# A hybrid retention, DeltaNet and MoE block on one core: where the first expert's conversions and the shared expert's chunks stand in the order of issue

## The chip, the cores and the metric

The kernel runs on one core of a Trainium2 chip, as one launch. The metric is the device time of that core in microseconds; lower is better. The engines are TensorE (PE; weight loads are shown as PEld), VectorE (DVE), ScalarE (ACT), GpSimd (POOL) and SyncE (SP), each with an in-order queue of its own.

## The reference

One layer over 512 latent tokens of width 1024, with 256 context tokens. A token mixer (retention and gated DeltaNet) comes first and ends in a projection by `w_o`. Then follows a mixture of experts, the part that the change touches:

```python
scores = jax.nn.sigmoid((xt @ w_router_l).astype(jnp.float32))
...                                   # 4 of 8 groups kept, then the 8 best of 64 experts per token
slot_tok = jnp.full((n_slots,), t, jnp.int32).at[slot].set((order // TOP_K).astype(jnp.int32))
...
def expert_block(args):
    xe, e = args
    return (jax.nn.silu(xe @ w_gate_l[e]) * (xe @ w_up_l[e])) @ w_down_l[e]
...
shared = (jax.nn.silu(xt @ w_sh_gate_l) * (xt @ w_sh_up_l)) @ w_sh_down_l
return (routed + shared).reshape(b, l, d)
```

So each token goes to 8 of 64 experts (width 256) and to one shared expert (width 256); the two results are added, normed and added to the stream.

## The kernel before

Everything up to about 600 us is the token mixer. `phaseO` then does the last projection and the routing, in four tiles of 128 tokens. `proj(us, t, c)` (L1081) multiplies with `w_o`; `post(t)` (L1094) norms the tile on DVE, POOL and ACT into `h2`; `turn(t)` (L1112) transposes `h2` on TensorE (L1117), copies it to `h2T` on ACT (L1118) and calls `router(t)` (L1006): 8 matmuls (L1010), a sigmoid on ACT (L1012), then some 30 short DVE steps that end in the 0/1 selection `sel` (L1034) and the weights `wt`, which SP writes to DRAM. After every second tile `router` also transposes two selections into `selT` on TensorE (L1043).

The shared expert is done in four chunks of 128 tokens. `shared_up(t)` (L1051) is 32 matmuls on TensorE (64 records, L1056), a Silu on ACT (L1059) and a product on DVE (L1060); `shared_down(t)` (L1062) is 4 matmuls (8 records, L1067), two copies on ACT (L1068) and a DMA on the ACT queue. Chunk 0 runs in `phaseO`, chunks 1 to 3 in `phaseM`.

`phaseM` first places the lists: from `selT` and a table `left`, eight rounds of max and replace on DVE (L1193, L1195) give the first slots of every expert for two halves of the tokens; two copies put the halves into `both` (L1197 on ACT, L1198 on DVE), one small matmul brings them together (L1200) and DVE writes the token indices `slots` (L1202). With them `prepare(e)` gathers the tokens of an expert with an indirect DMA on POOL (L1214).

The weights of an expert come as three loads of 1 MB on the SP queue (L1178). Gate and up lie in a ring of six buffers (three experts); two of the six are the memory of `h2T`, and the third `w_down` buffer is that of the shared expert's `w_sh_down`, so that these come free only when the shared expert is done. A gate or up matrix is converted: `conv` (L1153) casts it on ACT into a high part `wh` (L1156) and subtracts on DVE into a low part `wl` (L1158); seven such buffers exist. `convert(e, n)` (L1263) does this for matrix n of expert e and then issues the load of expert e + 3 into the buffer that has come free. `make(e, part)` transposes the gathered tokens (L1222, with L1224 on ACT and L1225 on DVE). The loop over 64 experts (L1402) then does for each: the gate projection (L111 to L113), a conversion for the next expert, the transposes of the activations of the one before (L1242), the up projection, another conversion, the next `make`, `down` (L1253) with a scatter on POOL (L1258), and the next gather.

The order on each engine is not quite the order of the program text: a planner goes through the program with times of its own and may issue an instruction earlier than an earlier one in the text, if its inputs and buffers are free by its reckoning. So the three conversions that stand ahead of the loop in the text (experts 0, 0 and 1) and one from inside the loop run, in part, among the steps of `phaseO`. `tc.issue_after(ins)` is an order to that planner: every instruction made inside the block that runs on the engine of `ins` is queued behind `ins`; it puts no wait on the chip, and other engines are not bound by it.

Of the kernel before, what the change touches and what calls it, by code (L numbers as in the profile page):

```python
# [9 lines left out]
F32 = mybir.dt.float32  # L10
# [3 lines left out]
AF = mybir.ActivationFunctionType  # L14
OP = mybir.AluOpType
# [56 lines left out]
class K:  # L72
# [903 lines left out]
    def phaseO(self):  # L976
        nc, tc, a = self.nc, self.tc, self.a
        tt = nc.vector.tensor_tensor
        ts = nc.vector.tensor_scalar
# [7 lines left out]
        p = rt = self.pool("op", side="right", es=es, reuse=True)  # L987
# [10 lines left out]
        sc, cand, sel, wt, posm, rep, selb = G("scr"), G("cand"), G("sel"), G("wt"), G("posm"), G("rep"), G("selb", BF)  # L998
# [7 lines left out]
        def router(t):  # L1006

            ps = self.pi()
            for k in range(8):
                nc.tensor.matmul(ps[:, 0:64], self.h2T[:, k, t * 128:t * 128 + 128], wr[:, k], start=k == 0, stop=k == 7)  # L1010
            s, c = sc[:, t], cand[:, t]
            nc.scalar.activation(s, ps[:, 0:64], AF.Sigmoid)  # L1012
            tt(c, s, bias, op=OP.add)
            for g in range(8):
                nc.vector.max(t8[:, g], c[:, g * 8:g * 8 + 8])
            gs, kp, kb, m8, sm = [sm8[:, t, i * 8:i * 8 + 8] for i in range(5)]
            tt(gs, t8[:, :, 0], t8[:, :, 1], op=OP.add)
            i0 = gs[:, None, :].to_broadcast([128, 8, 8])
            i1 = gs[:, :, None].to_broadcast([128, 8, 8])
            tt(A, i0, i1, op=OP.is_gt)  # L1020
            tt(B, i0, i1, op=OP.is_equal)
            f = lambda x: x.rearrange("p g h -> p (g h)")
            tt(f(B), f(B), cons["glt"], op=OP.mult)
            tt(A, A, B, op=OP.add)
            nc.vector.tensor_reduce(kp, A, axis=AX.X, op=OP.add)
            ts(kp, kp, 3.5, None, op0=OP.is_lt)
            ts(kb, kp, -1.0, 1e30, op0=OP.add, op1=OP.mult)
            c3 = c.rearrange("p (g e) -> p g e", g=8)
            b8 = lambda x: x[:, :, None].to_broadcast([128, 8, 8])
            tt(c3, c3, b8(kp), op=OP.mult)  # L1030
            tt(c3, c3, b8(kb), op=OP.add)
            nc.vector.max(m8, c)
            nc.vector.match_replace(rep[:, t], m8, c, -3e30)
            tt(sel[:, t], rep[:, t], c, op=OP.not_equal)  # L1034
            tt(wt[:, t], s, sel[:, t], op=OP.mult)
            nc.vector.tensor_reduce(sm[:, 0:1], wt[:, t], axis=AX.X, op=OP.add)
            nc.vector.reciprocal(sm[:, 0:1], sm[:, 0:1])
            ts(wt[:, t], wt[:, t], sm[:, 0:1], 2.5, op0=OP.mult, op1=OP.mult)
            nc.vector.tensor_copy(selb[:, t], sel[:, t])
            nc.sync.dma_start(self.h2d[t * 128:t * 128 + 128, 1024:1088], wt[:, t])  # L1040

            if t % 2:
                nc.tensor.transpose(self.selT[:, t // 2 * 128:t // 2 * 128 + 128], sel[:, t - 1:t + 1].rearrange("p c e -> p (c e)"), self.ident)  # L1043


        b1, k0_ = self.hxpool.tile([128, 2, 8, 256], F32, name="wsh", tag="b1"), self.keep.tile([128, 2, 1024], F32, name="wshd", tag="k0")
        wsh = [b1[:, 0], b1[:, 1], k0_]
# [3 lines left out]
        def shared_up(t):  # L1051
            ts_ = slice(t * 128, t * 128 + 128)
            ps = self.pi()
            for j in range(4):
                for k in range(8):
                    nc.tensor.matmul(ps[:, j * 128:j * 128 + 128], wsh[j // 2][:, k, j % 2 * 128:j % 2 * 128 + 128], self.h2T[:, k, ts_],  # L1056
                                     start=k == 0, stop=k == 7)
            sg = sgs[t] = mp.tile([128, 256], F32, name="shg", bufs=2)
            nc.scalar.activation(sg, ps[:, 0:256], AF.Silu)  # L1059
            tt(sg, sg, ps[:, 256:512], op=OP.mult)  # L1060

        def shared_down(t):  # L1062
            y = self.rawp.tile([128, 1024], F32, name="y", tag="raw")
            for c in range(2):
                ps = self.pa()
                for k in range(2):
                    nc.tensor.matmul(ps, sgs[t][:, k * 128:k * 128 + 128], wsh[2][:, k, c * 512:c * 512 + 512], start=k == 0, stop=k == 1)  # L1067
                nc.scalar.copy(y[:, c * 512:c * 512 + 512], ps)  # L1068
            nc.scalar.dma_start(self.accd[0][t * 128:t * 128 + 128], y)

        self.shared = lambda t: (shared_up(t), shared_down(t))

        wo = a["w_o"][0].rearrange("(k p) n -> p k n", p=128)
# [38 lines left out]
        def turn(t):  # L1112
            for cc in range(2):
                ps = self.pi()
                for k in range(4):
                    kk = cc * 4 + k
                    nc.tensor.transpose(ps[:, k * 128:k * 128 + 128], h2s[t][:, kk * 128:kk * 128 + 128], self.ident)  # L1117
                nc.scalar.copy(self.h2T[:, cc * 4:cc * 4 + 4, t * 128:t * 128 + 128], ps.rearrange("p (k n) -> p k n", k=4))  # L1118
            router(t)
# [7 lines left out]
        for t in range(4):  # L1127
            proj(us, t, 1)
            post(t)
            if 0 < t < 3:  # L1130
                turn(t - 1)
        shared_up(0)
        turn(2)
        turn(3)
        shared_down(0)
        z = self.rawp.tile([128, 1024], F32, name="zero", tag="raw")
        nc.gpsimd.memset(z, 0.0)
        for t in range(4):
# [4 lines left out]
    def phaseM(self):  # L1143
        nc, tc, a = self.nc, self.tc, self.a
        tt = nc.vector.tensor_tensor
        ts = nc.vector.tensor_scalar
        p, cons, sel, selb, wt, posm = self.mp, self.cons, self.sel, self.selb, self.wt, self.posm
# [5 lines left out]
        def conv(w, eng, n):  # L1153
            h, l = T8("wh"), T8("wl")
            for i in range(0, 2048, max(n, 1024)):
                nc.scalar.copy(h[:, i:i + max(n, 1024)], w[:, i:i + max(n, 1024)])  # L1156
            for i in range(0, 2048, n):
                eng(l[:, i:i + n], w[:, i:i + n], h[:, i:i + n].bitcast(F32), op=OP.subtract)  # L1158
            return h, l
# [8 lines left out]
        raw = lambda e, n: DW[e % 3] if n == 2 else GU[(2 * e + n) % 6]  # L1168

        def load(e, n, wix=None):  # L1170
            if e > NE:
                return
            t = raw(e, n)
            if e == NE:
                wix = self.xtra[0] if wix is None else wix
                nc.gpsimd.indirect_dma_start(t[:, :], None, wf[NAMES3[n]], bass.IndirectOffsetOnAxis(ap=wix[:, :1], axis=0))
            else:
                nc.sync.dma_start(t, a[NAMES3[n]][0, e].rearrange("(p k) f -> p (k f)", p=128))  # L1178
# [2 lines left out]
            load(e, n)  # L1181


        lf = self.rawp.tile([128, 448], F32, name="left", tag="raw")
        left, first, both = lf[:, 0:256], lf[:, 256:320], lf[:, 320:448]
        o = self.coff["left"][0]
        nc.scalar.dma_start(left, a["cst"][:, o:o + 256])
# [2 lines left out]
        slots = p.tile([128, 64], I32, name="slots")  # L1190
        for r in range(8):
            e8 = first[:, r * 8:r * 8 + 8]
            nc.vector.max(e8, left)  # L1193
            if r < 7:
                nc.vector.match_replace(left, e8, left, 0.0)  # L1195

        nc.scalar.copy(both[0:64, 0:64], first[0:64])  # L1197
        nc.vector.tensor_copy(both[64:128, 64:128], first[64:128])  # L1198
        ps = self.pi()
        nc.tensor.matmul(ps[:, 0:64], both, cst("i2"), start=True, stop=True)  # L1200

        ts(slots, ps[:, 0:64], -1.0, 512.0, op0=OP.mult, op1=OP.add)  # L1202
        for t in range(1, 4):
            self.shared(t)
        xg6, xg3 = q.tile([128, 3, 1088], F32, name="xg", bufs=1), self.hxpool.tile([128, 3, 1088], F32, name="xg", tag="b1")
        xgs = [x[:, i] for x in (xg6, xg3) for i in range(3)]
        for x in xgs:
# [55 lines left out]
        def convert(e, n):  # L1263
            if e <= NE:
                cv[e, n] = conv(raw(e, n), tt, 2048)
                load(e + 3, n)
# [3 lines left out]
        def prepare(e):  # L1270

            if e > NE:
                return
            if e < NE:
                SL[e] = slots[:, e:e + 1]
            else:
                SL[e], W[e] = self.xtra[1:]
            XG[e] = gather(SL[e])
            if e < NE:
                W[e] = XG[e][:, 1024 + e:1025 + e]  # L1280
# [7 lines left out]

        for e in range(3):
            prepare(e)  # L1290
        convert(0, 0)
        convert(0, 1)
        convert(1, 0)
        for e in range(2):
            make(e, 0)
            make(e, 1)
# [8 lines left out]
        ps = self.pi()  # L1305
# [10 lines left out]
        for t in range(4):  # L1316
            s = slice(t * 64, t * 64 + 64)
# [166 lines left out]
```

## Time and profile before

| what | us |
|---|---|
| median of 3 runs | 1450.79 (1450.4 to 1452.89) |
| the profiled execution | 1450.15 |
| its span, first to last instruction | 1448.4 |
| TensorE busy | 1338.8 (92% of the span) |
| DVE busy | 901.3 (62%) |
| ACT busy | 655.7 (45%) |
| POOL busy | 404.1 (28%) |

The busy shares are means over stages that differ: the mixer to about 600 us, the routing from there to about 736 us, the expert loop to about 1413 us, and the last sums. The rows below come from the routing and from the loop. A timeline row gives the start, the duration of the merged instructions, engine, line, operation, the tile written and those read, and the count; in brackets stands how long the engine was idle before it, and which instruction ended that. A granted clock of 1.00 is 2.4 GHz and 0.50 is 1.2 GHz.

### The profile page before, as it was taken

What the parts mean: (1) busy time and instruction counts of PE and PEld (TensorE: products, weight loads), DVE (VectorE), ACT (ScalarE), POOL (GpSimd) and SP (SyncE); (2) the same over time, 40 slices, a digit from 0 to 9 for tenths busy, and PEclk for the clock granted to TensorE, in tenths of its full rate; (3) what the DMA queues carried; (4) which work ended last, traced back from release to release, by engine and by line L of the source; (5) the groups of instructions that cost most, each with busy time, mean ns of one, the idle gap of its engine ahead of it and who ended that gap; (6) DMA issues with size and microseconds to landing.
All of it is one profiled execution on the core that took longest, in us unless ns stands there. A gap on an engine that the chain in (4) does not pass through costs nothing.

```text
span 1448.4 us, 20720 instructions
## 1 busy us (share of the span) xinstructions
PE 1338.8 (92%) x7848; PEld 1085.2 (75%) x7848; DVE 901.3 (62%) x1268; ACT 655.7 (45%) x927; POOL 404.1 (28%) x330
## 2 busy tenths in 40 slices
PE   6989888899999999997799999999999999999991
PEld 2668776898887767776678787878787878888770
DVE  5635695566777556557366666666666666666543
ACT  5534442543323223244145655555555555555531
POOL 0414644855330000012022222222222222223312
PEclk9899999999999999999899999999999999999995
DMA  8643421102226578566388999999999999999954
GB/s 283 191 106 107 125 58 41 44 16 84 78 69 203 177 212 232 167 248 245 136 282 295 351 364 347 367 354 347 364 357 361 362 362 357 368 353 353 327 184 124
DMA packets 138841, 340.51 MB, mean 235 GB/s; under 512 B 28218, under 2 KB 84574, under 8 KB 113780
## 3 DMA queue, kind: packets, MB, share of 16 engines
q1 hardware_dynamic: 110952, 289.46, 56.5%
q0 software_dynamic: 19584, 38.99, 10.7%
q10 hardware_dynamic: 8204, 10.72, 2.4%
q8 instruction: 63, 1.03, 0.3%
q14 instruction: 38, 0.31, 0.1%
HBM read 326.59 MB, written 48.31 MB: 259 GB/s over the span
## 4 chain that ended last, share of the span: by engine, by line
PE 66%; DVE 8%; DMA 8%; POOL 2%; issue 2%; ACT 1%; SPq 0%; ACTq 0%; DVEq 0%; POOLq 0%
PE cs L1253 15%; PE acc L113 12%; PE acc L112 12%; PE acc L111 12%; PE ci L1222 4%; DMA raw<-in_w_in_dram 2%; PE ci L1056 2%; DMA wd<-in_w_down_dram 2%; DVE wu L107 1%; PE acc L1242 1%; PE acc L1067 1%; DMA mraw<-in_w_mod_dram 1%; ACT wu L100 1%; PE ci L596 1%; PE cs L655 1%
## 5 line engine op out<-in xcount | busy, mean ns | idle before, releaser
L111 PE MATMUL acc<-wh,xT 128*128 128x256 f32 x1040 | 304.9, 293 | 0.0
L113 PE MATMUL acc<-wh,xT 128*128 128x256 f32 x1040 | 294.4, 283 | 0.0
L112 PE MATMUL acc<-wl,xT 128*128 128x256 f32 x1040 | 294.1, 283 | 0.0
L1158 DVE TENSOR_TENSOR wl<-w,wh 128x2048 fp32r<-128x2048 f32 x88 | 201.6, 2291 | 87.4 <-PE acc L112 86.0
L1253 PE MATMUL cs<-wd,aT 128*128 128x512 f32 x520 | 235.8, 596 | 2.9 <-DMA wd<-in_w_down_dram 2.1
L1258 POOL DMA_INDIRECT acc<-y,slots x64 | 101.9, 1592 | 474.7 <-ACT y L1255 427.4
L1156 ACT CAST wh<-w 128x2048 fp32r<-128x2048 f32 x88 | 167.3, 1901 | 100.7 <-PE acc L113 85.6
L111 PEld LDWEIGHTS acc<-wh,xT 128*128 128x128 f32 x1040 | 199.6, 192 | 0.2 <-issue 0.2
L112 PEld LDWEIGHTS acc<-wl,xT 128*128 128x128 f32 x1040 | 199.4, 192 | 0.2 <-issue 0.2
L113 PEld LDWEIGHTS acc<-wh,xT 128*128 128x128 f32 x1040 | 198.8, 191 | 0.0
L1253 PEld LDWEIGHTS cs<-wd,aT 128*128 128x128 f32 x520 | 94.5, 192 | 97.6 <-issue 96.6
L1225 DVE TENSOR_TENSOR xT<-ci,xT 128x512 fp32r<-128x512 f32 x130 | 89.1, 686 | 89.7 <-ACT xT L1224 89.6
L100 ACT CAST wu<-raw 128x1024 fp32r<-128x1024 f32 (+1 forms) x73 | 74.9, 1036 | 113.4 <-DMA raw<-in_w_in_dram 74.1
L1158 DVE TENSOR_TENSOR wl<-wgu,wh 128x2048 fp32r<-128x2048 f32 x42 | 96.3, 2292 | 41.5 <-PE acc L112 41.4
L111 PE MATMUL acc<-hTx,wu 128*128 128x512 f32 (+1 forms) x296 | 119.2, 403 | 1.9 <-ACT wu L100 1.9
L113 PE MATMUL acc<-hTx,wu 128*128 128x512 f32 (+1 forms) x296 | 118.4, 400 | 1.5 <-DVE wu L107 1.5
L112 PE MATMUL acc<-hLx,wu 128*128 128x512 f32 (+1 forms) x296 | 117.9, 398 | 0.0
L107 DVE TENSOR_TENSOR wu<-raw,wu 128x1024 fp32r<-128x1024 f32 (+1 forms) x61 | 77.1, 1270 | 64.6 <-ACT wu L100 63.5
L1156 ACT CAST wh<-wgu 128x2048 fp32r<-128x2048 f32 x42 | 79.7, 1898 | 50.0 <-PE acc L113 42.1
L1222 PEld LDWEIGHTS ci<-ident,xg 128*128 128x128 f32 x520 | 73.4, 192 | 29.8 <-issue 29.5
L1214 POOL DMA_INDIRECT xg<-h2d,slots x64 | 71.3, 1113 | 31.6 <-issue 18.0
L1222 PE MATMUL ci<-ident,xg 128*128 128x128 f32 x520 | 80.0, 278 | 0.0
(492 smaller groups left out, 2371.6 us busy)
## 6 DMA issues: line engine op xcount, KB each, us to landing
wd<-in_w_down_dram SPq DMA_DIRECT2D x64, 1024.0 KB
w<-in_w_gate_dram SPq DMA_DIRECT2D x43, 1024.0 KB
w<-in_w_up_dram SPq DMA_DIRECT2D x43, 1024.0 KB
raw<-in_w_in_dram SPq DMA_DIRECT2D x56, 512.0 KB
wgu<-in_w_gate_dram SPq DMA_DIRECT2D x21, 1024.0 KB
wgu<-in_w_up_dram SPq DMA_DIRECT2D x21, 1024.0 KB
mraw<-in_w_mod_dram SPq DMA_DIRECT2D x32, 512.0 KB
wm<-in_w_mod_dram SPq DMA_DIRECT2D x16, 512.0 KB
```

The source lines that it names most:

```text
L100: nc.scalar.copy(dst, src)
L107: (self.nc.gpsimd if eng == "pool" else self.nc.vector).tensor_tensor(dst, src, hi.bitcast(F32), op=OP.subtract)
L111: mm(out, ah, bh, start=start, stop=False)
L112: mm(out, ah, bl, start=False, stop=False)
L113: mm(out, al, bh, start=False, stop=stop)
L1156: nc.scalar.copy(h[:, i:i + max(n, 1024)], w[:, i:i + max(n, 1024)])
L1158: eng(l[:, i:i + n], w[:, i:i + n], h[:, i:i + n].bitcast(F32), op=OP.subtract)
L1214: nc.gpsimd.indirect_dma_start(xg[:, :], None, self.h2d[:, :], bass.IndirectOffsetOnAxis(ap=ix, axis=0), bounds_check=511, oob_is_err=False)
L1222: nc.tensor.transpose(ps[:, k * 128:k * 128 + 128], xv[:, :, c * 4 + k], self.ident)
L1225: tt(l, ps, h.bitcast(F32), op=OP.subtract)
L1253: nc.tensor.matmul(ps, aT[:, m], wd[:, s], start=k == 0, stop=k == 1)
L1258: nc.gpsimd.indirect_dma_start(self.accd[acc][:, :], bass.IndirectOffsetOnAxis(ap=sx, axis=0), y[:, :], None, bounds_check=511, oob_is_err ...
```

## The change

In `phaseO` the transposes of the selections are taken out of `router` into `turn_sel`. `shared_up(1)` now follows `shared_down(0)`; the two `turn_sel` are queued on TensorE behind its last matmul, and `shared_down(1)` follows. In `phaseM` `shared(2)` stands between the eight rounds and the copies into `both`; the first of these copies moves from ACT to DVE. The table `left` moves from the ring `raw`, which the shared expert's results use too, to a buffer `k1`. `shared(3)` and the three conversions ahead of the loop stand in a block whose ACT instructions are queued behind the last router's sigmoid and whose DVE instructions are queued behind the writing of `slots`; `shared(3)` stands behind the first of the conversions.

```diff
@@ -1009,7 +1009,7 @@
             for k in range(8):
                 nc.tensor.matmul(ps[:, 0:64], self.h2T[:, k, t * 128:t * 128 + 128], wr[:, k], start=k == 0, stop=k == 7)
             s, c = sc[:, t], cand[:, t]
-            nc.scalar.activation(s, ps[:, 0:64], AF.Sigmoid)
+            self.scored = nc.scalar.activation(s, ps[:, 0:64], AF.Sigmoid)
             tt(c, s, bias, op=OP.add)
             for g in range(8):
                 nc.vector.max(t8[:, g], c[:, g * 8:g * 8 + 8])
@@ -1039,8 +1039,9 @@
             nc.vector.tensor_copy(selb[:, t], sel[:, t])
             nc.sync.dma_start(self.h2d[t * 128:t * 128 + 128, 1024:1088], wt[:, t])
 
-            if t % 2:
-                nc.tensor.transpose(self.selT[:, t // 2 * 128:t // 2 * 128 + 128], sel[:, t - 1:t + 1].rearrange("p c e -> p (c e)"), self.ident)
+        def turn_sel(t):
+
+            nc.tensor.transpose(self.selT[:, t // 2 * 128:t // 2 * 128 + 128], sel[:, t:t + 2].rearrange("p c e -> p (c e)"), self.ident)
 
 
         b1, k0_ = self.hxpool.tile([128, 2, 8, 256], F32, name="wsh", tag="b1"), self.keep.tile([128, 2, 1024], F32, name="wshd", tag="k0")
@@ -1053,11 +1054,12 @@
             ps = self.pi()
             for j in range(4):
                 for k in range(8):
-                    nc.tensor.matmul(ps[:, j * 128:j * 128 + 128], wsh[j // 2][:, k, j % 2 * 128:j % 2 * 128 + 128], self.h2T[:, k, ts_],
-                                     start=k == 0, stop=k == 7)
+                    mm = nc.tensor.matmul(ps[:, j * 128:j * 128 + 128], wsh[j // 2][:, k, j % 2 * 128:j % 2 * 128 + 128], self.h2T[:, k, ts_],
+                                          start=k == 0, stop=k == 7)
             sg = sgs[t] = mp.tile([128, 256], F32, name="shg", bufs=2)
             nc.scalar.activation(sg, ps[:, 0:256], AF.Silu)
             tt(sg, sg, ps[:, 256:512], op=OP.mult)
+            return mm
 
         def shared_down(t):
             y = self.rawp.tile([128, 1024], F32, name="y", tag="raw")
@@ -1133,6 +1135,10 @@
         turn(2)
         turn(3)
         shared_down(0)
+        with tc.issue_after(shared_up(1).ins):
+            turn_sel(0)
+            turn_sel(2)
+        shared_down(1)
         z = self.rawp.tile([128, 1024], F32, name="zero", tag="raw")
         nc.gpsimd.memset(z, 0.0)
         for t in range(4):
@@ -1181,7 +1187,7 @@
             load(e, n)
 
 
-        lf = self.rawp.tile([128, 448], F32, name="left", tag="raw")
+        lf = self.keep.tile([128, 448], F32, name="left", tag="k1")
         left, first, both = lf[:, 0:256], lf[:, 256:320], lf[:, 320:448]
         o = self.coff["left"][0]
         nc.scalar.dma_start(left, a["cst"][:, o:o + 256])
@@ -1193,15 +1199,14 @@
             nc.vector.max(e8, left)
             if r < 7:
                 nc.vector.match_replace(left, e8, left, 0.0)
-
-        nc.scalar.copy(both[0:64, 0:64], first[0:64])
+        self.shared(2)
+
+        nc.vector.tensor_copy(both[0:64, 0:64], first[0:64])
         nc.vector.tensor_copy(both[64:128, 64:128], first[64:128])
         ps = self.pi()
         nc.tensor.matmul(ps[:, 0:64], both, cst("i2"), start=True, stop=True)
 
-        ts(slots, ps[:, 0:64], -1.0, 512.0, op0=OP.mult, op1=OP.add)
-        for t in range(1, 4):
-            self.shared(t)
+        listed = ts(slots, ps[:, 0:64], -1.0, 512.0, op0=OP.mult, op1=OP.add)
         xg6, xg3 = q.tile([128, 3, 1088], F32, name="xg", bufs=1), self.hxpool.tile([128, 3, 1088], F32, name="xg", tag="b1")
         xgs = [x[:, i] for x in (xg6, xg3) for i in range(3)]
         for x in xgs:
@@ -1288,9 +1293,12 @@
 
         for e in range(3):
             prepare(e)
-        convert(0, 0)
-        convert(0, 1)
-        convert(1, 0)
+
+        with tc.issue_after(self.scored.ins), tc.issue_after(listed.ins):
+            convert(0, 0)
+            self.shared(3)
+            convert(0, 1)
+            convert(1, 0)
         for e in range(2):
             make(e, 0)
             make(e, 1)
```

## Rows read from the trace of the kernel before

**Rows 1.** by stretch: us, busy us of each engine, granted clock, DMA share, GB/s

```profile
695.00:700.00 5.00, 0.89 (x4) 0.92 (x5) 3.70 (x13) 1.34 (x2) 0.00 (x0) 0.50 0.89 374
700.00:705.00 5.00, 5.00 (x26) 5.00 (x25) 0.03 (x1) 0.19 (x1) 3.16 (x3) 0.50 0.23 58
832.24:842.56 10.32, 10.32 (x69) 8.40 (x68) 6.87 (x6) 6.00 (x8) 2.62 (x2) 1.00 1.00 349
```

**Rows 2.** one tile's instructions, `wh`: ns min/median/max, first and last start

```profile
L111 PEld LDWEIGHTS acc<-wh,xT x1040: 187/192/337, 736.4 to 1407.9; 128*128 128x128 f32 x174
```

**Rows 3.** waits of TensorE, 600 to 680 us: us in total, times, longest

```profile
PE cs L1043 <- DVE sel L1034: 4.3, 1, 4.3
...
PE ci L1117 <- DVE shg L1060: 1.7, 1, 1.7
...
PE ci L1117 <- DVE rB L1023: 0.7, 1, 0.7
```

**Rows 4.** waits of TensorE, 680 to 760 us

```profile
PE ci L1200 <- ACT left L1197: 8.4, 1, 8.4
PE cs L1043 <- DVE sel L1034: 3.9, 1, 3.9
PE ci L1362 <- DVE colx L1348: 3.2, 1, 3.2
```

**Rows 5.** timeline of TensorE, 662 to 745 us: start, us, engine, line, operation, tiles

```profile
668.73 1.04 PE L1117 MATMUL ci<-ident,h 128*128 128x128 f32 x8
...
679.25 1.70 PE L1117 MATMUL ci<-ident,h 128*128 128x128 f32 x7
...
699.56 12.56 PE L1056 MATMUL ci<-h2T,wsh 128*128 128x128 f32 x86
711.96 3.60 PE L1067 MATMUL acc<-wshd,shg 128*128 128x512 f32 x8
...
724.71 6.19 PE L1056 MATMUL ci<-h2T,wsh 128*128 128x128 f32 x54
```

**Rows 6.** timeline of DVE, 662 to 711 us (idle before, and what ended it)

```profile
666.18 2.28 DVE L1158 TENSOR_TENSOR wl<-w,wh 128x2048 fp32r<-128x2048 f32 x1
...
675.71 1.29 DVE L1108 SCALAR_TENSOR_TENSOR h<-h,rr,mrow 128x1024 f32<-128x1024 f32 x1 [0.66 <-POOL rr L127]
...
690.09 0.22 DVE L1034 TENSOR_TENSOR sel<-rep,cand 128x64 f32<-128x64 f32 x1
...
699.80 0.22 DVE L1202 TENSOR_SCALAR slots<-ci 128x64 int32<-128x64 f32 x1 [0.95 <-PE ci L1200]
710.12 0.42 DVE L1060 TENSOR_TENSOR shg<-shg,ci 128x256 f32<-128x256 f32 x1 [10.09 <-ACT shg L1059]
```

**Rows 7.** timeline of ACT, 668 to 699 us

```profile
668.41 1.90 ACT L1156 CAST wh<-w 128x2048 fp32r<-128x2048 f32 x1 [4.09 <-DMA w<-in_w_up_dram]
...
673.51 1.07 ACT L1118 COPY h2T<-ci 128x512 f32<-128x512 f32 x2
...
684.73 0.22 ACT L1012 ACTIVATE scr<-ci 128x64 f32<-128x64 f32 x1 [1.15 <-DMA left<-in_cst_dram]
...
698.64 0.24 ACT L1197 COPY left<-left 64x64 f32<-64x64 f32 x1 [11.55 <-DVE left L1193]
```

**Rows 8.** timeline of the SP queue, the third early load

```profile
675.43 0.38 SPq L1178 DMA_DIRECT2D w<-in_w_gate_dram  x1
```

**Rows 9.** waits of TensorE, 760 us to the end

```profile
PE cs L1253 <- DMA wd<-in_w_down_dram: 2.1, 1, 2.1
```

**Rows 10.** timeline of POOL: the first gather, and one late in the loop

```profile
700.91 1.16 POOL L1214 DMA_INDIRECT xg<-h2d,slots  x1 [12.57 <-DVE slots L1202]
...
1309.42 3.11 POOL L1214 DMA_INDIRECT xg<-h2d,slots  x1 [0.30 <-PE acc L113]
```

**Rows 11.** timeline of DVE at that late gather

```profile
1309.33 2.29 DVE L1158 TENSOR_TENSOR wl<-wgu,wh 128x2048 fp32r<-128x2048 f32 x1 [1.31 <-PE acc L112]
```

**Rows 12.** the gathers' tile `xg`: from issue to landing

```profile
DMA to landing us min/median/max: 3.5/11.0/12.8
```

## The prediction

> **What bounds the kernel now.** First I read the busy time by stretch. In the expert loop a stretch of 10.32 us holds 10.32 us of TensorE work at the full clock, 2.4 GHz, while the DMA share is 1.00 as well [rows 1]. So there TensorE sets the pace, the loop is 64 times that period, and whatever moves the loop's start moves the end by the same amount, unless the period itself changes. The first expert's projection begins at 736.4 us [rows 2], right behind the last transposes of the stage ahead of it. The stage before that is the other picture: between 695 and 700 us TensorE worked 0.89 us out of 5 at a clock of 0.50 (1.2 GHz), and the next 5 us of solid work still ran at 0.50 [rows 1].
>
> Second, who TensorE waits for there: in the part up to 680 us 4.3 us for the selection `sel` (L1043), 1.7 us at the transposes L1117 after the shared expert's DVE product, and 0.7 us at L1117 behind a router step [rows 3]; after that 8.4 us for the list of tokens (L1200) and 3.9 us for the second `sel` [rows 4]. The 3.2 us at L1362 [rows 4] lie inside the first two experts; the change doesn't touch them. TensorE's queue runs in order, so the first L1043 also holds back router(2), which needs nothing from it.
>
> Third, what could have stood in those gaps: three chunks of the shared expert run after the list instead, 64 matmul records each. At the full clock 54 records take 6.19 us, 0.1146 each, so a chunk's first half takes 7.3 us and its second half 3.60 us [rows 5]: 10.9 us a chunk, 32.7 us for three, all of it between the list and the loop, on a TensorE that the list does not need.
>
> **The change part by part.**
>
> *Chunks 1 and 2 into the gaps.* The work is the same; only its place moves. The list itself takes from `sel` at 690.09 to `slots` at 699.80, 9.7 us of short DVE steps [rows 6]. Now shared_down(0), shared_up(1) (7.3) stand before the transposes of the selections, and shared_down(1), shared(2) (3.6 + 10.9 = 14.5 us) beside those 9.7 us. The waits 8.4 and 3.9 are filled: **12.3 us**. What is late next is then TensorE itself: the list is ready before it has finished shared(2), so L1200 may stand up to 3.6 us behind shared_down(2). That costs nothing, since no time of TensorE is lost and shared(3), 10.9 us, is left to cover the gathers.
>
> *The selections' transposes out of router(t).* The head of the queue is free: of 4.3 + 1.7 + 0.7 = 6.7 us what remains is the chain's own latency. I put the rest at 3.1 us: twice the copies of h2T at 1.07 us [rows 7], in which TensorE has only the router's work, and about 1 us for the last h2. Gain **3.6 us**; the bounds are 0 (the gaps merely change their name) and 6.7 (a chunk is planned into them too).
>
> *The clock.* The 86 records after the list took 12.56 us instead of 86 x 0.1146 = 9.9, and 7 transposes 1.70 instead of 7/8 of 1.04 = 0.9 [rows 5]: 2.7 + 0.8 = **3.5 us** spent at 1.2 GHz. Without long idle the clock should hold; for the 3.1 us that remain I take 0.5 off.
>
> *The three conversions.* They now leave the router's chain: on DVE two subtractions (one of the two is shown, 2.28 us) stood in the last token tile's chain, which ends with its h2 at 675.71 [rows 6], and on ACT a cast stood until 670.3 after 4.09 us for its load, with the copies of h2T behind it [rows 7]. Those 4.6 us of DVE bring the last router forward; it is what makes the 3.6 us above possible and isn't counted again. What they cost in the new place: ACT 3 x 1.9 us behind the last sigmoid, where ACT idled 11.55 us [rows 7]; DVE 3 x 2.28 = 6.9 us behind `slots`, where DVE had nothing for 10.09 us and more [rows 6]. The first projection needs only one of them, done 2.4 us after `slots`, while TensorE has shared(3) for 10.9 us. Cost 0; without that cover up to 6.9 us. Should `slots` come so late that the subtractions run into the loop, the wait at L1362, which hangs on DVE, grows from 3.2 us [rows 4] by as much.
>
> *Their loads.* Each conversion issues on SP the load three experts on. The last was issued at 675.43 [rows 8]; all three now come after `slots`, ahead of or between the loads of expert 2, which wait for shared_up(3) anyway. It is 3 x 1.05 MB at 349 GB/s [rows 1], 9 us of lead that the loop no longer has. In the whole loop TensorE waited 2.1 us for a weight [rows 9], and a buffer is refilled three periods, 31 us, before its use. I take 0; bound 0 to 9 us.
>
> *POOL.* The three first gathers (1.16 us for the first [rows 10]) follow `slots` as before; the memsets of the later three buffers wait for shared_up(3), also as before. The new neighbour is DVE: a gather that began 0.09 us after a subtraction of 2.29 us took 3.11 us [rows 10, 11]. So the first gather may come 2.0 us late; if it loses to all three subtractions, 6.9 us. Its data are wanted some 7.3 us after `slots` (shared_up(3)), so 2 us stay hidden, 6.9 would show as about 4. I take 0, being nearest to the row. The Trainium skill (SBUF — State Buffer, "SBUF: two separate sides") calls the port pair that VectorE and GpSimd share an exclusive lock: whichever starts first keeps it for its whole instruction. The trace agrees, 3.11 us against 1.16; by the rule the later case below is open, by the row alone the sum stays.
>
> *Small ones.* `left` no longer waits in the raw ring: the last sigmoid stood 1.15 us behind its DMA [rows 7], and this is part of the chain above. The copy moved from ACT (0.24 us) to DVE saves a hop, 0.1 to 0.3 us, hidden behind shared(2). A new wait of the same kind: DVE's product of chunk 2 stands before those copies, so the list may wait for shared_up(2); it is the 3.6 us case above. Silu and product between the halves of a chunk (0.42 us on DVE [rows 6], as much on ACT) cost about **1 us** in all where no other matmul is planned between.
>
> Sum: 12.3 + 3.6 + 3.5 - 0.5 - 1.0 = 17.9, say **18 us**. The profiled execution has a span of 1448.4 us and took 1450.15; the median of the runs is 1450.79. 1448.4 - 18 = 1430.4, plus 1.75 around the span, plus 0.64 from this run to the median: **1432.8 us**.
>
> **The rivals.**
>
> *A foreign conversion takes the place.* Only three conversions are held back. That of expert 1's second matrix isn't, and its cast is the one at 668.41 that waited for its load [rows 7]. If it stays there, the copies of h2T remain behind 670.3, and with buffers now free its subtraction (2.28 us) can enter the router's chain. Price 2.3 + about 2 us: gain 13 to 14, 1437. For it: no edge forbids it. Against: before, it stood behind the three in the ring of buffers.
>
> *The list ends up behind all chunks on TensorE.* Nothing holds shared(3)'s matmuls behind L1200. Then `slots` come after 10.9 us more, and gathers, transposes and the subtractions are bare: about 1 us from `slots` to the gather, at least 3.5 from its issue to its landing [rows 12], an estimated 2 to 3 for transposes and copies (like the 1.04 and 1.07 us of h2's [rows 5, 7]), some 7 us idle, with 1 to 2 at the low clock. Gain 9 to 11, 1441. Against: the list's steps are ready first.
>
> *The port.* The first gather loses to all three subtractions: 4 us on TensorE before the transposes, 1437. The lock rule cited above allows it; the row shows one subtraction lost, not three.
>
> *Nothing happens:* the order planned before and after leaves the same gaps, 1450.
>
> *The other side: transfers set the loop's pace.* The lead of 9 us is gone and DMA share is 1.00. If the transfers can't bring an expert's data in 10.32 us, the period grows. 18 us over 64 experts are 0.28 us: it decides from a period of 10.60, or 340 GB/s instead of 349. At 335 GB/s it is 10.75 us, 64 x 0.43 = 27.5 us, so 9.5 us slower than before: 1460. Against: the 2.1 us above, and the load per expert is unchanged, so only a lead is lost, not a rate.
>
> **How the numbers follow.** The forecast, 1426 to 1438, 0.60: from a gain of 24 (all of 6.7 filled, part of the 3.2 us too) to 13. Foreign conversion 0.13, port 0.06, list behind all chunks 0.11; nothing 0.04; slower 0.06. The range 1425 to 1441 takes in the forecast and most of the partial cases, about 0.85. Faster by over 0.2% (2.9 us, about what a measurement of this kernel can tell from no change) 0.90; within it 0.04; slower 0.06.
>
> **What would show it.** Right: TensorE without the waits at L1200 and L1043; the shared matmuls at 0.115 us a record throughout; the first expert's projection near 718 us; the conversions' subtractions directly behind `slots`; the loop's period still 10.32. Wrong in its steps: a cast or subtraction of experts ahead of the last sigmoid or of `slots`; a wait of the first transposes (L1222) for a gather; `slots` later than 707; casts that wait for loads in the first experts; a period over 10.4, which would overturn the whole forecast.

## The result and the profile after

The changed kernel takes 1427.8 us (median of 4, 1426.8 to 1430.6) against 1450.6 us for the kernel before in the same set: a ratio of 0.984, 95% interval 0.983 to 0.986, so 22.8 us less. The forecast was 1432.8 us. The profiled execution has a span of 1426.5 us, 21.9 less than before.

Where the time went is read from two cuts. The last stretch of work that the change cannot touch is the projection by `w_o`; its first matmul, the first expert's projection and the last expert's stand in two rows of the view of the tile `acc` (ns min/median/max of one, first and last start); the experts' row comes first. Before:

```profile
L111 PE MATMUL acc<-wh,xT x1040: 277/283/681, 736.4 to 1408.0; 128*128 128x256 f32 x174
...
L111 PE MATMUL acc<-wu,mh x64: 387/389/480, 608.0 to 660.9; 128*128 128x512 f32 x64
```

After:

```profile
L111 PE MATMUL acc<-wh,xT x1040: 278/283/681, 712.2 to 1385.0; 128*128 128x256 f32 x174
...
L111 PE MATMUL acc<-wu,mh x64: 387/389/477, 607.3 to 659.6; 128*128 128x512 f32 x64
```

The routing stage, from the first start of the `w_o` projection to that of the experts', shrank from 128.4 to 104.9 us, **23.5 us**. The loop, from the first expert projection to the last, grew from 671.6 to 672.8 (+1.2), what follows it from 40.4 to 41.5 (+1.1), and the mixer ended 0.7 earlier: -23.5 + 1.2 + 1.1 - 0.7 = -21.9. The last term is no effect of the change: in the ten profiles of this study the `w_o` projection begins anywhere from 605.4 to 610.0. So a start in the loop is compared by its distance from that point, not by its time in the span.

The stage by stretch, cut where the `w_o` projection ends (us, busy us of PE, PEld, DVE, ACT, POOL, granted clock, DMA share, GB/s). Before, and then after:

```profile
661.60:736.40 74.80, 56.52 (x363) 47.53 (x362) 32.24 (x128) 19.74 (x31) 14.84 (x16) 0.86 0.47 174
```

```profile
660.40:712.20 51.80, 50.68 (x364) 42.40 (x362) 34.69 (x125) 22.71 (x32) 18.09 (x15) 1.00 0.71 269
```

TensorE's idle time fell from 18.3 to 1.1 us, and the same work (363 and 364 records) took 5.8 us less, at a granted clock of 1.00 instead of 0.86. That is 23.0 of the 23.5; the rest lies inside the `w_o` projection, where the wait of 0.7 us of [rows 3] stood (at 654.5). What is left of the waits in the stretch, from the view of 600 to 680 us (two more, of 1.7 and 1.3 us, lie inside the `w_o` projection, before and after alike):

```profile
PE ci L1010 <- ACT h2T L1120: 0.8, 1, 0.8
PE ci L1119 <- DVE shg L1061: 0.3, 1, 0.3
```

The waits for the list (L1207 now) and for the selections (L1044) are gone against [rows 3, 4]. The timeline of TensorE shows what stands in their place; the rows answer to [rows 5]:

```profile
669.29 1.10 PE L1010 MATMUL ci<-wr,h2T 128*128 128x64 f32 x8 [0.79 <-ACT h2T L1120]
...
671.68 0.93 PE L1119 MATMUL ci<-ident,h 128*128 128x128 f32 x7
...
677.67 7.31 PE L1057 MATMUL ci<-h2T,wsh 128*128 128x128 f32 x64
684.82 0.38 PE L1044 MATMUL cs<-ident,sel 128*128 128x128 f32 x2
685.04 2.62 PE L1057 MATMUL ci<-h2T,wsh 128*128 128x128 f32 x22
...
695.71 0.33 PE L1207 MATMUL ci<-c_i,left 128*128 128x64 f32 x2
...
706.51 1.04 PE L1227 MATMUL ci<-ident,xg 128*128 128x128 f32 x8
```

Where the waits for the selections and for the list stood there is now a chunk's work, at 0.114 to 0.119 us a record in these rows, and the 7 transposes take 0.93 instead of 1.70 us. The list's matmul runs in the middle of a chunk, and the first tokens' transposes (L1227) follow without a wait.

What was not gained shows in the first experts, as waits of TensorE from 680 to 760 us and on ACT's timeline there:

```profile
PE ci L1370 <- DVE colx L1356: 3.9, 1, 3.9
PE cs L1258 <- ACT aT L1249: 0.3, 1, 0.3
```

```profile
716.79 1.91 ACT L1162 CAST wh<-wgu 128x2048 fp32r<-128x2048 f32 x1 [3.87 <-DMA wgu<-in_w_gate_dram]
720.98 1.91 ACT L1162 CAST wh<-wgu 128x2048 fp32r<-128x2048 f32 x1 [2.01 <-DMA wgu<-in_w_up_dram]
```

Both casts of expert 2 now stand behind their loads, and the wait for `colx` grew from 3.2 [rows 4] to 3.9 us.

### The profile page after: what moved, and what is told of

Same layout as the page of the kernel before. It is cut to its first block, busy times and chain, and to the rows that moved or that the text cites. A ratio compares the mean times of both kernels' runs of the same rounds, so it can differ in the third digit from the quotient of the medians.

```text
span 1426.5 us, 20707 instructions
## 1 busy us (share of the span) xinstructions
PE 1334.9 (94%) x7848; PEld 1081.8 (76%) x7848; DVE 901.3 (63%) x1269; ACT 654.1 (46%) x926; POOL 404.4 (28%) x330
## 4 chain that ended last, share of the span: by engine, by line
PE 46%; DMA 5%; DVE 1%; POOL 1%; issue 0%; ACT 0%; DVEq 0%; SPq 0%; POOLq 0%; ACTq 0%
PE cs L1258 15%; PE acc L112 8%; PE acc L111 8%; PE acc L113 8%; PE ci L1227 4%; DMA wd<-in_w_down_dram 2%; PE ci L1057 2%; DMA wgu<-in_w_up_dram 1%; PE acc L1247 1%; PE acc L1069 1%; DMA w<-acc 1%; POOL fr L127 0%; DMA acc<-y,sl_i 0%; DMA acc<-y,slots 0%; PE ci L1010 0%
## 5 line engine op out<-in xcount | busy, mean ns | idle before, releaser
L1164 DVE TENSOR_TENSOR wl<-wgu,wh 128x2048 fp32r<-128x2048 f32 x42 | 96.3, 2292 | 42.7 <-PE acc L112 41.5
L1227 PEld LDWEIGHTS ci<-ident,xg 128*128 128x128 f32 x520 | 73.6, 192 | 29.9 <-issue 29.5
L1219 POOL DMA_INDIRECT xg<-h2d,slots x64 | 71.5, 1117 | 35.6 <-issue 18.3
L1227 PE MATMUL ci<-ident,xg 128*128 128x128 f32 x520 | 80.4, 279 | 0.0
```

The source lines that it names most:

```text
L1219: nc.gpsimd.indirect_dma_start(xg[:, :], None, self.h2d[:, :], bass.IndirectOffsetOnAxis(ap=ix, axis=0), bounds_check=511, oob_is_err=False)
L1227: nc.tensor.transpose(ps[:, k * 128:k * 128 + 128], xv[:, :, c * 4 + k], self.ident)
```

## The experiments

The kernel before, the change and the eight experiments, cut at the same three points (us, of the profiled execution; the last column is the median of the runs). The ratios below go by runs of the kernel before on the same chip, with a median of 1449.6 for experiments 1 to 4 and 1450.2 for 5 to 8.

| kernel | ahead of the stage | stage | loop | rest | span | median |
|---|---|---|---|---|---|---|
| before | 608.0 | 128.4 | 671.6 | 40.4 | 1448.4 | 1450.6 |
| the change | 607.3 | 104.9 | 672.8 | 41.5 | 1426.5 | 1427.8 |
| 1 conversions alone | 607.2 | 122.7 | 669.6 | 40.7 | 1440.2 | 1441.8 |
| 2 chunks alone | 610.0 | 112.5 | 669.9 | 41.3 | 1433.7 | 1434.0 |
| 3 transposes back in the router | 608.3 | 109.9 | 671.2 | 41.1 | 1430.5 | 1431.3 |
| 4 extra expert's steps later | 609.4 | 104.8 | 664.6 | 41.1 | 1419.9 | 1421.4 |
| 5 list behind all chunks | 607.1 | 120.3 | 669.3 | 40.6 | 1437.3 | 1442.1 |
| 6 edit 4 on the kernel before | 605.4 | 128.1 | 665.2 | 39.6 | 1438.3 | 1442.5 |
| 7 early loads later | 608.3 | 104.9 | 670.9 | 40.9 | 1425.0 | 1425.2 |
| 8 edits 4 and 7 | 606.6 | 106.6 | 664.7 | 41.4 | 1419.3 | 1421.1 |

**1. The conversions alone**, on the kernel before:

```diff
-            nc.scalar.activation(s, ps[:, 0:64], AF.Sigmoid)
+            self.scored = nc.scalar.activation(s, ps[:, 0:64], AF.Sigmoid)
...
-        ts(slots, ps[:, 0:64], -1.0, 512.0, op0=OP.mult, op1=OP.add)
+        listed = ts(slots, ps[:, 0:64], -1.0, 512.0, op0=OP.mult, op1=OP.add)
...
-        convert(0, 0)
-        convert(0, 1)
-        convert(1, 0)
+        with tc.issue_after(self.scored.ins), tc.issue_after(listed.ins):
+            convert(0, 0)
+            convert(0, 1)
+            convert(1, 0)
```

> The kernel before with one part of the change: the three conversions queued behind the last sigmoid (ACT) and behind slots (DVE); chunks 1 to 3 of the shared expert and the transposes of the selections stay where they were. Theory (what counts is TensorE's idle time, and the chunks fill most of it): the last router comes some 8 us earlier, but TensorE still stands about 4.4 us for the second selection and 8.4 us for the list, and the 2.7 us of slow clock behind it stay; of 19.0 us of waits about 15.6 are left, so 3.5 to 6 us faster than before, 1445 to 1447. Rival (the conversions in the router's chain are the larger part of the gain, the chunks the smaller): 12 us or more faster, under 1439.

Measured: ratio 0.994 (0.993 to 0.996), 7.8 us less by the medians, more than the 3.5 to 6 that I expected; the stage alone gained 5.7. The loop, 2.0 shorter, and the mixer's end, 0.8 earlier, make the rest of the span's 8.2; why the loop was shorter was not traced. The rival (12 us or more) is out. TensorE's waits from 600 to 680 us:

```profile
PE cs L1043 <- DVE sel L1034: 2.0, 1, 2.0
PE ci L1117 <- DVE h L1108: 1.7, 1, 1.7
PE acc L112 <- DVE wu L107: 1.3, 1, 1.3
PE ci L1010 <- ACT h2T L1118: 0.2, 1, 0.2
```

Against [rows 3] 4.3 + 1.7 + 0.7 became 2.0 + 0.2: the conversions were what made the router late, and taking them out alone is worth 4.5 us there and about one at the clock. With them gone the planner also put the first selection's transpose into the middle of `shared_up(0)`, so the 4.5 us hold that move too. The waits of [rows 4] are as before, 8.4 and 3.9, and of the clock's part 0.8 us lies behind them, where TensorE's order is the same as before: the 86 records of [rows 5] after the same 8.41 us of idle took 11.75 instead of 12.56 us.

```profile
693.82 11.75 PE L1056 MATMUL ci<-h2T,wsh 128*128 128x128 f32 x86
```

**2. The chunks alone**, on the changed kernel:

```diff
-        with tc.issue_after(self.scored.ins), tc.issue_after(listed.ins):
+        if True:
```

> The changed kernel without its block around the three conversions: chunks 1 and 2 and the transposes stand as in the change, the conversions are free to run among the router's steps, as before. Theory: the waits of 8.4 and 3.9 us are gone and the clock holds behind the list, but the copies of h2T and the last h2 come as late as before, so about 4.3 + 1.7 us of TensorE's waits and 1 us of slow clock stay: 5 to 8 us slower than the changed kernel, 1433 to 1436. First rival (the chunks alone do it): within 2 us of the changed kernel. Second rival (the conversions are the larger part): 12 us or more slower than the changed kernel, over 1440.

Measured: ratio 0.988 (0.986 to 0.990), as expected. The stage gained 15.9 of the 23.5 us. What it lacks is one wait and the clock behind it: TensorE's timeline there reads

```profile
676.19 3.68 PE L1010 MATMUL ci<-wr,h2T 128*128 128x64 f32 x16 [4.41 <-ACT h2T L1120]
```

The 16 matmuls after 4.41 us of idle took 3.68 us, against 1.89 at full clock in the changed kernel. Two conversions are behind that wait: the cast that stands in front of the copies of h2T on ACT, as in [rows 7], and a subtraction on DVE (668.23 to 670.51), behind which DVE's `mix` comes late, which ACT wants next:

```profile
670.36 1.90 ACT L1162 CAST wh<-w 128x2048 fp32r<-128x2048 f32 x1 [4.03 <-DMA w<-in_w_up_dram]
672.82 1.06 ACT L1108 ACTIVATE ojunk<-mix 128x1024 bf16<-128x1024 f32 x1 [0.55 <-DVE mix L1103]
```

15.9 + 5.7 = 21.6 of 23.5: the two parts of the change add up but for about 2 us. Those lie at the clock: TensorE's busy time in the stage fell by 1.6 us in experiment 1, by 2.2 here and by 5.8 with both. But experiment 8, which leaves the order of the stage as it is in the change, saved only 4.2, so most of the 2 us may be the scatter of one execution. The new buffer of `left` and the copy moved to DVE are part of this experiment; no run takes them apart from the chunks.

**3. The selections' transposes back in the router**, on the changed kernel:

```diff
+            if t % 2:
+                turn_sel(t - 1)
...
-        with tc.issue_after(shared_up(1).ins):
-            turn_sel(0)
-            turn_sel(2)
+        shared_up(1)
```

> The changed kernel with the two transposes of the selections back in the router of tiles 1 and 3, without an order behind shared_up(1); all else as in the change. In the planned order they then stand in the middle of shared_up(0) and behind 13 matmuls of shared_up(1). Theory (TensorE waits at the head of its queue): about 2 us for the first selection and 1.5 for the second, while the list starts some 2.5 us earlier, which is worth nothing since TensorE has chunks to do: 2 to 5 us slower than the changed kernel, 1430 to 1433. Rival (the list is the path that counts): up to 2.5 us faster.

Measured: ratio 0.987 (0.985 to 0.989), and 5.0 us more in the stage than the change. TensorE's waits there, 3.4 us for the selections again:

```profile
PE cs L1047 <- DVE sel L1034: 3.4, 2, 2.0
```

With the smaller ones its waits are 3.0 us more than the change's, and TensorE's busy time is 1.9 us more at a clock of 0.97: together the 5.0. So of the 23.5 us this small edit carries about 5, as expected, and the rival (the list is the path that counts) is out.

**4. The extra expert's steps later**, on the changed kernel:

```diff
-        self.xtra = extra()
         x = lambda e: [XT[e][:, h] for h in range(2)]
         for e in range(NE + 2):
+            if e == 4:
+                self.xtra = extra()
```

> The changed kernel with the first search for overflowing experts (the call of extra, whose one-hot matmuls stand in TensorE's queue ahead of expert 2's transposes) moved from ahead of the loop to expert 4. If the 3.9 us that TensorE waits there for colx, and the stretch at about 0.6 of the clock behind it, come from DVE being full at that point, both go: 4 to 6 us faster than the changed kernel, 1422 to 1424. If the wait only moves to the later place, or another wait stands right behind it: no change, within 1.5 us.

Measured: 1421.4 us, ratio 0.981 (0.979 to 0.983), a little better than the 1422 to 1424 expected. The loop is 8.2 us shorter than in the changed kernel. TensorE's idle time in it fell from 6.5 to 1.8 us, with the wait of 3.9 gone and none for `colx` later; its busy time fell from 666.3 to 662.8 us, and that is the clock, which in the changed kernel was 0.73 from 730 to 735 us and 0.59 in the next 5, and is 1.00 here. This is a kernel that beats both.

**5. The list behind all chunks**, on the changed kernel, so that nothing covers the gathers:

```diff
         self.shared(2)
+        last = self.shared(3)[1]
...
-        nc.tensor.matmul(ps[:, 0:64], both, cst("i2"), start=True, stop=True)
+        with tc.issue_after(last.ins):
+            nc.tensor.matmul(ps[:, 0:64], both, cst("i2"), start=True, stop=True)
...
             convert(0, 0)
-            self.shared(3)
```

(`shared_down` returns its last matmul for this.)

> The changed kernel with the list's small matmul queued on TensorE behind the last matmul of shared(3), so that no chunk is left to cover the gathers. My account (the 10.9 us of shared(3) hide the slots, the gathers of 2.5 us and the landing of their data): slots come some 0.6 us after the end of shared(3) near 706, the gather's data some 5 us after that, transposes and copies run at a clock of 0.50, the first projection stands 7 to 9 us later than the 712.2 of the changed kernel; the wait for colx may give back up to 3 us of it, as the conversions then have more lead. 1432 to 1437. The rival (the conversions on ACT and DVE set the loop's start, the gathers do not): the first projection within 2 us of 712, 1426 to 1430.

Measured: 1442.1 us, ratio 0.995 (0.993 to 0.997), worse than the 1432 to 1437 that I expected. The rival is out, and my account had a size wrong by a factor of two: the stage is 15.4 us longer, of which TensorE waits 10.82 for the first gather and 1.25 for the second.

```profile
723.49 1.94 PE L1230 MATMUL ci<-ident,xg 128*128 128x128 f32 x8 [10.82 <-DMA xg<-h2d,slots]
```

The gather was issued at 713.81. From issue to landing the tile's view gives, for it alone and for it with the two behind it (min/median/max):

```profile
DMA to landing us min/median/max: 9.5/9.5/9.5
...
DMA to landing us min/median/max: 9.5/10.1/11.2
```

Before, the same gathers took 3.5 to 3.7. What differs is the traffic: here the weight loads of expert 2 and the three early ones are on their way at the same time (422 GB/s from 720 to 725 us), while before almost nothing was (58 GB/s, [rows 1]). That the loads are the cause is shown by experiment 7.

**6. Edit 4 on the kernel before:**

```diff
-        self.xtra = extra()
...
+            if e == 4:
+                self.xtra = extra()
```

> The kernel before, with the extra expert's preparation (self.xtra = extra()) moved from ahead of the loop to its fifth pass. Theory: the wait for colx is old, its price is the wait of 3.2 us and the low clock behind it, and the change only lengthened it by 0.7 us: 1444 to 1447, 4 to 7 us faster than before. Rival (the 6.5 us that the same edit brought on the changed kernel come from the lead that the loads lost there): gain of at most 2 us, 1448.5 to 1451.

Measured: ratio 0.995 (0.993 to 0.997), 7.7 us less by the medians, faster than the 1444 to 1447 that I gave; the rival (2 us at most) is out. The span is 10.1 less, but the two rows of its tile `acc` take 2.6 of that away again:

```profile
L111 PE MATMUL acc<-wh,xT x1040: 278/283/681, 733.5 to 1398.7; 128*128 128x256 f32 x174
...
L111 PE MATMUL acc<-wu,mh x64: 388/389/473, 605.4 to 658.3; 128*128 128x512 f32 x64
```

The mixer, which the edit doesn't touch, was 2.6 us earlier in this execution; the loop itself is 6.4 shorter. So the wait for `colx` was worth 6.4 us before the change (3.2 of waiting, as much of clock) and 8.2 after it: the theory holds, the change lengthened an old wait.

**7. The three early loads behind those of expert 2**, on the changed kernel:

```diff
-                nc.sync.dma_start(t, a[NAMES3[n]][0, e].rearrange("(p k) f -> p (k f)", p=128))
+                loads[e, n] = nc.sync.dma_start(t, a[NAMES3[n]][0, e].rearrange("(p k) f -> p (k f)", p=128))
...
-                load(e + 3, n)
+                if e + 3 <= NE:
+                    with tc.issue_after(loads[2, 1].ins):
+                        load(e + 3, n)
```

> The changed kernel with the three loads that the conversions ahead of the loop issue (experts 3, 3 and 4) queued on SP behind those of expert 2, so that expert 2's come some 8 us earlier and the three some 9 us later. Theory (lead costs only the part of the wait for colx that grew, and nothing else): the casts of expert 2 no longer wait for DMA, the wait for colx is back at about 3.2 us, the first projection stays at 712, 1426 to 1429. Rival (lead is short everywhere, the three loads are late in their turn): casts of expert 3 wait for DMA and TensorE with them, 1430 to 1437.

Measured: 1425.2 us, ratio 0.983 (0.980 to 0.986), just below the 1426 to 1429 expected; by time it can't be told from the change. The trace can: the casts of expert 2 no longer wait for their loads, and of the 3.9 us for `colx` 1.7 are left, but a wait of 1.5 for `aT` is new:

```profile
PE ci L1374 <- DVE colx L1360: 1.7, 1, 1.7
PE cs L1260 <- ACT aT L1251: 1.5, 1, 1.5
```

The new wait is the rival in a small form. A cast of expert 3 waits 2.96 us for its load, the copy of `aT` stands behind it on ACT, and TensorE waits for that copy:

```profile
724.73 1.90 ACT L1162 CAST wh<-w 128x2048 fp32r<-128x2048 f32 x1 [2.96 <-DMA w<-in_w_gate_dram]
726.53 0.36 ACT L1251 COPY aT<-acc 128x256 f32<-128x256 f32 x1
```

As a whole the loop is 1.9 us shorter than with the change, so the rival's price (1430 to 1437) did not come. And the gathers, with no weight load issued from 686 to 707 us, land sooner (min/median/max of the first three); the second row is experiment 4, where the loads stand as in the changed kernel:

```profile
DMA to landing us min/median/max: 4.5/4.5/5.2
```

```profile
DMA to landing us min/median/max: 8.4/9.7/11.3
```

**8. The edits of 4 and 7 together**, on the changed kernel:

> Both edits on the changed kernel: the extra expert's preparation in the fifth pass, and the three loads queued behind those of expert 2. Theory (without the wait for colx the lead costs TensorE nothing, wherever it goes): as with the first edit alone, 1420 to 1423. Rival (with 6 us less of cover the loads of expert 3 come too late): 1424 or more, with a wait of TensorE in L111 or L112 between 730 and 760.

Measured: 1421.1 us, ratio 0.981 (0.978 to 0.983), as expected: the same as edit 4 alone, with no wait of TensorE between 712 and 760 us. Without the wait for `colx` the lost lead costs nothing that shows.

## Why the prediction was right, and where it was off

**The mechanism was right**: waits on the router and on the list were filled by work that stood bare behind them, the clock rose with it, and the loop's pace stayed: 240 us of it, from 60 us behind its start, hold 240.00 us of TensorE work before and after. The first expert's projection, forecast near 718 us, came at 712.2. Term by term for the stage:

| term | forecast | measured |
|---|---|---|
| waits 8.4 + 3.9 | 12.3 | 12.3 |
| waits 4.3 + 1.7 + 0.7 | 3.6 | 5.6 |
| Silu and product between halves | -1.0 | 0 |
| clock | 3.5 - 0.5 = 3.0 | 5.8 |
| sum | 17.9 | 23.7 by waits and busy time, 23.5 by starts |
| loop and rest | 0 | -2.3 |

The 1.1 us by which the part behind the loop grew were not traced.

- *The rest of the head of the queue* was put at 3.1 us and is 1.1: while ACT copies one h2T, TensorE transposes the next tile or runs the chunk's other half, so only 0.8 and 0.3 stay. The upper bound 6.7 was nearer than the value taken.
- *The 1.0 for Silu and product* was charged for a case that doesn't occur: 22 records of the next chunk stand between the halves (the row at 685.04).
- *The clock* was the term most wrong. The forecast counted the two groups of [rows 5] that were visibly slow. But all of the stage's busy time at 0.50 counts, and its short groups too: the router's matmuls, the shared_down ones and the transposes of `sel` among them. Two rows of TensorE's timeline before,

```profile
674.21 1.52 PE L1010 MATMUL ci<-wr,h2T 128*128 128x64 f32 x8
...
677.65 1.81 PE L1010 MATMUL ci<-wr,h2T 128*128 128x64 f32 x8
```

  took 1.10 and 1.00 after. The sign of it was in the stretch's own row: a mean clock of 0.86 is 28% of 74.8 us, 20.9 us, at 0.50, and whatever of that is busy costs half its length. Every record in it had to be set against its duration at 1.00. Part of the size is chance all the same: experiment 8 gives 4.2 where the change gives 5.8.
- *The conversions' new place* was free, as forecast, for TensorE: their subtractions stand right behind `slots`, and the first projection waits for none of them. Their *loads' lost lead* was taken as 0 of a bound of 9. Two casts of expert 2 are late, one of the signs of a wrong step that the prediction had named, and through DVE the wait for `colx` is 0.7 us longer than before. In the loop's length that is 1.2 us against before and 2.9 against experiment 2, which has the lead; but experiment 3, with the first of these loads issued 13.5 us ahead of the first projection as in the change, and the same 3.9 us for `colx`, has a loop of 671.2 us, shorter than before. So beyond the 0.7 us the price is within what executions differ by. The prediction named that wait as the place where lateness would show, but tied it to late `slots`, not to late loads.
- *The port.* The three gathers next to the subtractions took 2.47, 2.08 and 1.87 us; in experiment 2, where no subtraction is near, 1.16, 1.01 and 0.99, as in [rows 10].

```profile
697.19 2.47 POOL L1219 DMA_INDIRECT xg<-h2d,slots  x1 [16.53 <-DVE slots L1209]
699.96 2.08 POOL L1219 DMA_INDIRECT xg<-h2d,slots  x1 [0.30 <-issue]
702.35 1.87 POOL L1219 DMA_INDIRECT xg<-h2d,slots  x1 [0.30 <-issue]
```

```profile
696.34 2.29 DVE L1164 TENSOR_TENSOR wl<-w,wh 128x2048 fp32r<-128x2048 f32 x1
698.88 4.49 DVE L1164 TENSOR_TENSOR wl<-w,wh 128x2048 fp32r<-128x2048 f32 x2
```

  The first lost 1.3 us, not 6.9, so the case in which it loses to all three subtractions did not come about. Each gather ends about 1 us after the end of the subtraction that ran as it began (698.63 and 699.66 for the first). That is what the exclusive lock in the Trainium skill (SBUF — State Buffer, "SBUF: two separate sides") would give for the gather. But the second subtraction began at 698.88, while the first gather still ran, and was no longer than one alone (2.25 against 2.28 us): as far as the profile's spans on POOL, which are rough, can tell, a lock for the gather's whole instruction does not show.
- *The cover for the gathers* was the step that was right by luck. It was reckoned with 2 us of port and 3.5 of landing. The changed kernel's trace has no landing for these gathers. In experiment 4, whose order of loads is the same, it took 8.4 for the first: issued at 699.21, there at 707.6, and the transposes that need it start at 708.54. So 0.9 us was left of a cover that seemed ample. The early loads are what lengthened it (5.2 us without them, in experiment 7), a cost that the prediction looked for on TensorE's weights and not on the gathers.
- *The rivals.* The foreign conversion stayed behind its ring: cast at 702.13, subtracted at 716.48. "List behind all chunks" was priced at 1441, and forced in experiment 5 it gave 1442.1, but not as priced: the gather landed in 9.5 us instead of 3.5. The transfers did not set the loop's pace.

## What to carry to other kernels

Cost a low clock by all the records of the stretch that had it, not by the groups that look slow. When a step that issues loads is moved, ask which small transfers will then be on their way beside them and who waits for those. And set two profiles against each other at the last point that the change can't reach; here that point itself moved by up to 4.6 us between executions.

## What the runs showed of the hardware

From issue to landing the first three gathers took 8.4 to 11.3 us with weight loads of 1 MB issued between them (experiment 4), and 4.5 to 5.2 with these loads moved behind them (experiment 7): 3.2, 5.2 and 6.8 us less. What is left above the 3.5 to 3.7 of the kernel before is about what the gathers themselves were longer beside the subtractions (0.9 to 1.3 us). The Trainium skill (DMA: Bandwidth & Descriptors, "Queues, rings and completion order") says that an engine takes turns between its queues packet by packet. No run here shows those turns, nor where in the transfer the time goes.

The same short gaps left the clock alone in one execution and not in another. The changed kernel and experiment 8 have the same order of instructions on TensorE there and the same two waits of 0.8 and 0.3 us, as have experiments 4 and 7; in the change and in those two the next 7 transposes took 0.93 us, in experiment 8

```profile
671.18 1.70 PE L1119 MATMUL ci<-ident,h 128*128 128x128 f32 x7
```

and its stage is 1.7 us longer than the change's (granted clock 0.85 from 668 to 672 us and 0.72 in the next 4). What decided it is open.
